# Whole-slot instructions, one root per store, pairwise adds and a 120-partition first piece in an fp32 pooling kernel

## Chip, cores, metric

One core of one Trainium2 chip. The metric is device time in microseconds (us), as the median of several executions. Ratios compare the mean time of one kernel's fast runs with that of the kernel before in the same rounds, so a ratio is not quite the ratio of the medians quoted next to it.

## The reference

For p = 2 and windows of 4 the reference is a root mean square over each window of the last axis:

```
x: float32 [32, 256, 4096]                   # 134.2 MB
window = np.abs(x[:, :, start:start + 4]) ** 2
result[:, :, i] = np.mean(window, axis=-1) ** (1 / 2)   # float32 [32, 256, 1024], 33.6 MB
```

## The kernel before

The input is seen as 128 partitions of 262144 columns. Three input slots of 13184 columns rotate. A slot is loaded by one transfer and worked in three chunks: ScalarE (ACT) squares a chunk in place, VectorE (DVE) sums each four neighbours, ACT takes the root of the chunk before. Two loads make one output group, which leaves by one store.

```python
    slots = [[(W, [4416, 4384, 4384])]] * 18
    ...
        for step in chunks:
            v = xs[i][:, c:c + step]
            nc.scalar.activation(out=v, in_=v, func=Act.Square)
            ...
            nc.vector.tensor_reduce(
                out=o, in_=v.rearrange("p (n j) -> p n j", j=k),
                axis=mybir.AxisListType.X, op=mybir.AluOpType.add,
            )
            if pending is not None:
                root(*pending)
```

Loads are issued by the sync queue (SP), stores of groups 0 to 6 by ACT's queue. The last four stores (g7 to g10) are held back to the end of SP's queue, so that they fill the DMA engines while the last loads are computed.

Of the kernel before, what the change touches and what calls it, by code (L numbers as in the profile page):

```python
# [1 line left out]

# [4 lines left out]


@with_exitstack
def kernel(  # L10
    ctx: ExitStack,
    tc: tile.TileContext,
    x: bass.AP,
    p: float,
    kernel_size: int,
    out: bass.AP,
):






    nc = tc.nc

    assert float(p) == 2.0, "kernel specialized for p == 2"
    k = int(kernel_size)
    assert k == 4, "kernel specialized for kernel_size == 4"

    P = nc.NUM_PARTITIONS  # L30
    fp32 = mybir.dt.float32
    Act = mybir.ActivationFunctionType
    xf = x.rearrange("b c l -> (b c l)")
    of = out.rearrange("b c l -> (b c l)")
    total = xf.shape[0] // P

    W, O_W = 13184, 6592
    X_SLOTS, O_SLOTS = 3, 2
    slots = [[(W, [4416, 4384, 4384])]] * 18
    slots += [[(6592, [3296, 3296])] * 2, [(6592, [3296, 3296]), (5056, [2528, 2528])]]  # L40
    groups = [2] * 9 + [3, 1]
    late = {7, 8, 9, 10}
    in_x = {9, 10}


    loads = [(s, sum(w for w, _ in slot[:j]), *slot[j]) for s, slot in enumerate(slots)
             for j in range(len(slot))]
    n = len(loads)
    assert sum(w for _, _, w, _ in loads) == total

    firsts = [sum(groups[:g]) for g in range(len(groups))]
    assert sum(groups) == n
    group_of = [g for g, count in enumerate(groups) for _ in range(count)]
    columns = [sum(w for _, _, w, _ in loads[firsts[g]:firsts[g] + groups[g]])
               for g in range(len(groups))]

    x_pool = ctx.enter_context(tc.tile_pool(name="x_pool", bufs=X_SLOTS))
    o_pool = ctx.enter_context(tc.tile_pool(name="o_pool", bufs=O_SLOTS))
    ctx.enter_context(tc.manual_schedule())

    def block(flat, g, div):
        at, width = sum(columns[:g]) * P // div, columns[g] * P // div
        return flat[at:at + width].rearrange("(p w) -> p w", p=P)

    slot_tiles = {}
    xs = {}

    def load(i):
        s, at, w, _ = loads[i]
        if at == 0:  # L70
            slot_tiles[s] = x_pool.tile([P, W], fp32, name="xt")
        v = slot_tiles[s][:, at:at + w]
        g = group_of[i]
        src = sum(loads[j][2] for j in range(firsts[g], i))
        nc.sync.dma_start(out=v, in_=block(xf, g, 1)[:, src:src + w])  # L75
        xs[i] = v

    ots = {}

    def store(g, queue):  # L80
        queue.dma_start(out=block(of, g, k), in_=ots[g])  # L81

    def root(g, o, ends):
        nc.scalar.activation(out=o, in_=o, func=Act.Sqrt, scale=1.0 / k)  # L84
        if ends and g not in late:
            store(g, nc.scalar)

    ahead = 0
    while ahead < n and loads[ahead][0] < X_SLOTS - 1:
        load(ahead)  # L90
        ahead += 1
    pending = None
    for i in range(n):
        s, _, w, chunks = loads[i]
        while ahead < n and loads[ahead][0] < s + X_SLOTS:
            load(ahead)
            ahead += 1
        g = group_of[i]
        if i == firsts[g]:
            pool, width = (o_pool, O_W) if g not in in_x else (x_pool, W)  # L100
            t = pool.tile([P, width], fp32, name="ot" if g not in in_x else "xt")
            ots[g] = t[:, 0:columns[g] // k]
        at = sum(loads[j][2] for j in range(firsts[g], i)) // k
        assert sum(chunks) == w
        c = 0
        for step in chunks:
            v = xs[i][:, c:c + step]
            nc.scalar.activation(out=v, in_=v, func=Act.Square)  # L108
            o = ots[g][:, at + c // k:at + (c + step) // k]
            nc.vector.tensor_reduce(  # L110
                out=o, in_=v.rearrange("p (n j) -> p n j", j=k),
                axis=mybir.AxisListType.X, op=mybir.AluOpType.add,
            )
            if pending is not None:
                root(*pending)
            c += step
            pending = (g, o, i == firsts[g] + groups[g] - 1 and c == w)
    root(*pending)
    for g in sorted(late):
        store(g, nc.sync)  # L120


# [1 line left out]
_INS = ['x', 'p', 'kernel_size']  # L124
_OUTS = [((32, 256, 1024), 'float32')]

_NUMBERS = {'p': 2.0, 'kernel_size': 4}


# [26 lines left out]
```

## Time and profile before

| | before |
|---|---|
| time | 394.69 us (394.66 to 394.81, 3 runs) |
| bytes moved | 167.8 MB in 390.0 us of transfers |
| plateau | 433 GB/s |
| DVE, ACT busy | 282.4 us, 292.4 us |

The page's row of DMA digits is the mean busy share of 16 DMA engines, so "9" in all inner slices means that there is little left to win. One thing the average hides is whether the 16 engines end together. The trace of the kernel before has 16 completions of each of its 33 transfers (528 four-byte packets); I read them as one for each of the 16 engines, but the trace does not say which engine a completion belongs to. For nearly every load of the steady stretch one engine completes about 0.5 us after the median engine, and at the last store 0.60 us after it (391.62 against 392.22 us). I call this distance the **lag**.

### The profile page before, as it was taken

How to read it: one execution, taken by the hardware profiler on the slowest of the kernel's cores; microseconds unless marked ns; L12 is line 12 of the kernel's file. 1: busy time of each engine (PE TensorE's matmuls, PEld its weight loads, DVE VectorE, ACT ScalarE, POOL GpSimd, SP SyncE). 2: the span in 40 equal slices, each digit the busy share in tenths (PEclk: the TensorE clock that was granted, in tenths of full speed). 3: DMA queues.
4: the chain of work that ended last, by engine and by line, in shares of the span. 5: the costliest groups of instructions: out<-in, count | busy, mean ns of one | idle time of the engine just before them, and what ended most of it. 6: DMA issues, size and time to landing. Idle time of an engine off the chain costs nothing.

```text
span 393.0 us, 316 instructions
## 1 busy us (share of the span) xinstructions
DVE 282.4 (72%) x62; ACT 292.4 (74%) x126; POOL 0.2 (0%) x4
## 2 busy tenths in 40 slices
DVE  0068989494959495949594959595859686899992
ACT  1099986777786768686958695959595949899991
POOL 0000000000000000000000000000000000000000
DMA  8999999999999999999999999999999999999997
GB/s 344 429 429 440 429 424 381 443 459 429 413 440 435 429 427 432 429 440 441 437 448 421 432 462 435 392 429 472 429 413 451 425 429 429 424 429 427 438 429 329
DMA packets 4754, 167.79 MB, mean 427 GB/s; under 512 B 528, under 2 KB 528, under 8 KB 656
## 3 DMA queue, kind: packets, MB, share of 16 engines
q1 hardware_dynamic: 3744, 144.15, 85.3%
q10 hardware_dynamic: 1008, 23.63, 14.0%
q14 instruction: 2, 0.02, 0.0%
HBM read 134.22 MB, written 33.55 MB: 427 GB/s over the span
## 4 chain that ended last, share of the span: by engine, by line
DMA 62%; ACT 19%; DVE 14%; issue 2%; ACTq 0%; SPq 0%
DMA xt<-in_x_dram 62%; ACT xt L108 15%; DVE ot L110 11%; DVE xt L110 3%; ACT ot L84 3%; ACT xt L84 1%; ACTq L81 0%; SPq L75 0%; ACTq L108 0%
## 5 line engine op out<-in xcount | busy, mean ns | idle before, releaser
L110 DVE TENSOR_REDUCE ot<-xt 128x1096 f32<-128x4384 f32 (+1 forms) x54 | 255.4, 4731 | 102.7 <-ACT xt L108 102.4
L108 ACT ACTIVATE xt<-xt 128x4384 f32<-128x4384 f32 (+3 forms) x62 | 230.3, 3716 | 89.2 <-DMA xt<-in_x_dram 86.3
L84 ACT ACTIVATE ot<-ot 128x1096 f32<-128x1096 f32 (+1 forms) x54 | 59.8, 1108 | 1.8 <-DVE ot L110 0.9
L110 DVE TENSOR_REDUCE xt<-xt 128x824 f32<-128x3296 f32 (+1 forms) x8 | 27.0, 3384 | 1.3 <-ACT xt L108 1.2
L84 ACT ACTIVATE xt<-xt 128x824 f32<-128x824 f32 (+1 forms) x8 | 6.7, 841 | 3.0 <-DVE xt L110 2.9
L108 ACT ACT_TABLE_LOAD x1 | 1.3, 1283 | 0.7 <-PEq L137 0.7
L84 ACT ACT_TABLE_LOAD x1 | 1.3, 1283 | 0.0
L137 POOL MEMSET const-bfloat16-1.0<- 128x1 bf16 x1 | 0.1, 101 | 0.0
L137 POOL MEMSET const-uint8-127<- 128x1 uint8 x1 | 0.1, 101 | 0.0
L137 POOL MEMSET const-float32-0.0<- 128x1 f32 x1 | 0.1, 98 | 0.2 <-issue 0.2
L137 POOL MEMSET const-float32-1.0<- 128x1 f32 x1 | 0.1, 98 | 0.0
## 6 DMA issues: line engine op xcount, KB each, us to landing
xt<-in_x_dram SPq DMA_DIRECT2D x18, 6592.0 KB, 39.7
out_dram<-ot ACTq DMA_DIRECT2D x7, 3296.0 KB, 26.4
xt<-in_x_dram SPq DMA_DIRECT2D x3, 3296.0 KB, 24.6
out_dram<-ot SPq DMA_DIRECT2D x2, 3296.0 KB, 29.6
xt<-in_x_dram SPq DMA_DIRECT2D x1, 2528.0 KB, 26.4
out_dram<-xt SPq DMA_DIRECT2D x1, 2472.0 KB, 9.3
out_dram<-xt SPq DMA_DIRECT2D x1, 632.0 KB, 5.0
```

Source lines behind the costliest of these rows:

```text
L84: nc.scalar.activation(out=o, in_=o, func=Act.Sqrt, scale=1.0 / k)
L108: nc.scalar.activation(out=v, in_=v, func=Act.Square)
L110: nc.vector.tensor_reduce(out=o, in_=v.rearrange("p (n j) -> p n j", j=k), axis=mybir.AxisListType.X, op=mybir.AluOpType.add,)
L137: nc = _bacc.Bacc("TRN2", target_bir_lowering=False, num_devices=1)
```

## The change

The intent is fewer, larger instructions and a short tail. Loads are squared and summed whole; one root is taken per store; from load 15 on, the sum is two pairwise adds, so that the coarse tail still ends in time; and 840 of the columns are laid on 120 partitions and loaded first, which spares one of the 16 DMA engines a little work. The core of the diff (cut; the rest gives tiles fixed addresses and moves offsets):

```diff
-    slots = [[(W, [4416, 4384, 4384])]] * 18
-    slots += [[(6592, [3296, 3296])] * 2, [(6592, [3296, 3296]), (5056, [2528, 2528])]]
+    slots = [[(W, [W])]] * 16 + [[(W, [6592, 6592])]] * 2
+    slots += [[(6592, [6592]), (6592, [6592])], [(6592, [6592]), (4216, [2112, 2104])]]
+    ODD = 840
...
+        if i < PAIRS:          # PAIRS = 15; the tensor_reduce of before
...
+        nc.vector.tensor_tensor(out=h, in0=q[:, :, 0:2], in1=q[:, :, 2:4], op=add)
+        nc.vector.tensor_tensor(out=o, in0=h[:, :, 0], in1=h[:, :, 1], op=add)
...
+    Q = 120
+    odd = ODD * P // Q
+    t = o_tiles[1][0:Q, 0:odd]
+    nc.sync.dma_start(out=t, in_=xf[(total - ODD) * P:total * P].rearrange("(p w) -> p w", p=Q))
...
+            if ends or i in FINE or (i in ENDS and c == w):
+                pending.append((done - 1, g, ots[g][:, rooted:summed], ends))
```

More of the change, by code (lines that the diff above doesn't have):

```diff
@@ L38 @@
     X_SLOTS, O_SLOTS = 3, 2
-    slots = [[(W, [4416, 4384, 4384])]] * 18
-    slots += [[(6592, [3296, 3296])] * 2, [(6592, [3296, 3296]), (5056, [2528, 2528])]]
+    slots = [[(W, [W])]] * 16 + [[(W, [6592, 6592])]] * 2
+    slots += [[(6592, [6592]), (6592, [6592])], [(6592, [6592]), (4216, [2112, 2104])]]
+    ODD = 840
     groups = [2] * 9 + [3, 1]
     late = {7, 8, 9, 10}
-    in_x = {9, 10}
+    in_x = {9: (2, 0), 10: (2, 4944)}
+    FINE, ENDS, LAG = {21}, {19, 20}, 1
+    PAIRS = 15
     loads = [(s, sum(w for w, _ in slot[:j]), *slot[j]) for s, slot in enumerate(slots)
@@ L48 @@
     n = len(loads)
-    assert sum(w for _, _, w, _ in loads) == total
+    assert sum(w for _, _, w, _ in loads) + ODD == total
     firsts = [sum(groups[:g]) for g in range(len(groups))]
@@ L55 @@
                for g in range(len(groups))]
-    x_pool = ctx.enter_context(tc.tile_pool(name="x_pool", bufs=X_SLOTS))
-    o_pool = ctx.enter_context(tc.tile_pool(name="o_pool", bufs=O_SLOTS))
+    x_pool = ctx.enter_context(tc.tile_pool(name="x_pool", bufs=1))
+    o_pool = ctx.enter_context(tc.tile_pool(name="o_pool", bufs=1))
+    x_tiles = [x_pool.tile([P, W], fp32, name=f"xt{j}") for j in range(X_SLOTS)]
+    o_tiles = [o_pool.tile([P, O_W], fp32, name=f"ot{j}") for j in range(O_SLOTS)]
     ctx.enter_context(tc.manual_schedule())
@@ L63, in block @@
         return flat[at:at + width].rearrange("(p w) -> p w", p=P)
-    slot_tiles = {}
     xs = {}
@@ L69, in load @@
         s, at, w, _ = loads[i]
-        if at == 0:
-            slot_tiles[s] = x_pool.tile([P, W], fp32, name="xt")
-        v = slot_tiles[s][:, at:at + w]
+        v = x_tiles[s % X_SLOTS][:, at:at + w]
         g = group_of[i]
@@ L86, in root, with total_sum @@
             store(g, nc.scalar)
+    def total_sum(o, v, i):
+        add = mybir.AluOpType.add
+        if i < PAIRS:
+            nc.vector.tensor_reduce(
+                out=o, in_=v.rearrange("p (n j) -> p n j", j=k),
+                axis=mybir.AxisListType.X, op=add,
+            )
+            return
+        q = v.rearrange("p (n j) -> p n j", j=k)
+        front = v[:, 0:v.shape[1] // 2]
+        h = front.rearrange("p (n j) -> p n j", j=2)
+        nc.vector.tensor_tensor(out=h, in0=q[:, :, 0:2], in1=q[:, :, 2:4], op=add)
[4 more added lines that the diff above has]
+    nc.sync.dma_start(out=t, in_=xf[(total - ODD) * P:total * P].rearrange("(p w) -> p w", p=Q))
     ahead = 0
-    while ahead < n and loads[ahead][0] < X_SLOTS - 1:
+    while ahead < n and loads[ahead][0] < X_SLOTS:
         load(ahead)
         ahead += 1
-    pending = None
+    nc.vector.tensor_tensor(out=t, in0=t, in1=t, op=mybir.AluOpType.mult)
+    o = o_tiles[1][0:Q, odd:odd + odd // k]
+    nc.vector.tensor_reduce(
+        out=o, in_=t.rearrange("p (n j) -> p n j", j=k),
+        axis=mybir.AxisListType.X, op=mybir.AluOpType.add,
+    )
+    nc.scalar.activation(out=o, in_=o, func=Act.Sqrt, scale=1.0 / k)
+    nc.scalar.dma_start(
+        out=of[(total - ODD) * P // k:total * P // k].rearrange("(p w) -> p w", p=Q), in_=o,
+    )
+    pending = []
+    done = 0
     for i in range(n):
@@ L99 @@
         if i == firsts[g]:
-            pool, width = (o_pool, O_W) if g not in in_x else (x_pool, W)
-            t = pool.tile([P, width], fp32, name="ot" if g not in in_x else "xt")
-            ots[g] = t[:, 0:columns[g] // k]
-        at = sum(loads[j][2] for j in range(firsts[g], i)) // k
+            t, first = (o_tiles[g % O_SLOTS], 0) if g not in in_x else (x_tiles[in_x[g][0]], in_x[g][1])
+            ots[g] = t[:, first:first + columns[g] // k]
+            summed = rooted = 0
         assert sum(chunks) == w
@@ L108 @@
             nc.scalar.activation(out=v, in_=v, func=Act.Square)
-            o = ots[g][:, at + c // k:at + (c + step) // k]
-            nc.vector.tensor_reduce(
-                out=o, in_=v.rearrange("p (n j) -> p n j", j=k),
-                axis=mybir.AxisListType.X, op=mybir.AluOpType.add,
-            )
-            if pending is not None:
-                root(*pending)
-            c += step
-            pending = (g, o, i == firsts[g] + groups[g] - 1 and c == w)
-    root(*pending)
+            total_sum(ots[g][:, summed:summed + step // k], v, i)
+            while pending and pending[0][0] <= done - LAG:
+                root(*pending.pop(0)[1:])
+            done += 1
+            c += step
+            summed += step // k
+            ends = summed == columns[g] // k
+            if ends or i in FINE or (i in ENDS and c == w):
+                pending.append((done - 1, g, ots[g][:, rooted:summed], ends))
+                rooted = summed
+    for job in pending:
+        root(*job[1:])
     for g in sorted(late):
```

## The prediction

The 27 GB/s of one engine are 52736 bytes in 1947 ns, the median packet of the kernel before.

For squares and reduces, a straight line through two shapes of the kernel before is an estimate: squares of 3296 and 4384 took 2933 and 3843 ns, so 13184 takes 11.20 us, 6592 5.69 and 2112 1.94; reduces of the same two sizes took 3586 and 4719 ns, so 13184 takes 13.88 us. Roots are put on the line of the squares (6592: 5.69 us, 3296: 2.93, 1648: 1.56). How long an add takes was the author's estimate, since the kernel before has none; the two adds of 13184 inputs then took 7.03 + 3.59 = 10.62 us.

> **What bounds the kernel now.** I read the page first, then the DMA row in windows, then the groups by form, then the waits of the queue that issues loads, then the timeline of the tail.
>
> The page:
>
> ```profile
> span 393.0 us, 316 instructions
> DVE 282.4 (72%) x62; ACT 292.4 (74%) x126; POOL 0.2 (0%) x4
> DMA  8999999999999999999999999999999999999997
> HBM read 134.22 MB, written 33.55 MB: 427 GB/s over the span
> ```
>
> Neither compute engine is above 74%, while the DMA row is full in every slice but the first and last. The page's chain of waits gives DMA only 62% and puts ACT and DVE at 33% together. That must not be read as "a third of the time is compute": the chain follows one buffer through square, reduce, next load, while the other buffers keep the DMA engines busy. The stage table tells it better (from:to in us, then length, busy time of DVE, ACT, POOL, clock, DMA share, GB/s):
>
> ```profile
> 20.00:56.00 36.00, 29.68 (x7) 33.72 (x14) 0.00 (x0) 1.00 1.01 435
> 56.00:64.00 8.00, 7.44 (x2) 7.96 (x3) 0.00 (x0) 1.00 0.95 356
> 64.00:340.00 276.00, 201.63 (x44) 205.83 (x87) 0.00 (x0) 1.00 1.00 433
> 340.00:380.00 40.00, 37.69 (x10) 38.73 (x19) 0.00 (x0) 1.00 1.01 433
> 380.00:393.00 13.00, 5.92 (x3) 4.44 (x4) 0.00 (x0) 1.00 0.81 348
> ```
>
> The plateau is 433 GB/s with share 1.00. Three places fall below it: the start, 56 to 64 us (the first store begins at 55.6), and the last microseconds. I now count what can be won at all. 167.77 MB at 433 GB/s take 387.5 us. The packet records start at 1.7 us and end at 391.7 us, so transfers are under way for 390.0 us, and 2.5 us of that is loss. The first store's dent is some 1.0 to 1.4 of it (8 us x (1 - 356/433) = 1.4; packets are booked where they start, so a window's edge is worth some tenths). The rest is the slow first packets and engines that don't end together. The 1.7 us ahead, the 1.3 us after the last packet, and the 1.7 us between span (393.0) and measured time (394.69) belong to launch and completion; the change doesn't touch them. So **perfect transfers would give 394.7 - 2.5 = 392.2 us, a gain of 0.6%.**
>
> Of the compute rows I need the durations by shape, and the queue's waits:
>
> ```profile
> L110 DVE TENSOR_REDUCE ot<-xt 128x1096 f32<-128x4384 f32 x36 | 169.9, 4719 | 6.7 <-ACT xt L108 6.4
> L108 ACT ACTIVATE xt<-xt 128x4384 f32<-128x4384 f32 x36 | 138.3, 3843 | 2.9 <-ACT ot L84 2.9
> L84 ACT ACTIVATE ot<-ot 128x1096 f32<-128x1096 f32 x36 | 39.7, 1103 | 1.1 <-DVE ot L110 0.9
> ...
> SPq L75 <- DVE ot L110: 307.7, 17, 18.7
> ```
>
> The load queue waits 17 times for a reduce to free a slot. This is harmless as long as the other two slots are still filling when the next load is issued.
>
> The tail in the timeline:
>
> ```profile
> 381.39 6.11 SPq L81 DMA_DIRECT2D out_dram<-xt  x2
> 386.42 0.73 ACT L84 ACTIVATE xt<-xt 128x632 f32<-128x632 f32 x1 [2.23 <-DVE xt L110]
> ```
>
> The last two stores are issued at 381.4 and, after the last root, at 387.2 us. Both are queued while earlier stores still drain, so the DMA does not run dry.
>
> [...]
>
> **The change part by part.**
>
> *Whole-slot instructions.* [...]Fewer fixed costs: ACT's squares and roots go from 124 to 39, [...]all on an engine that is not the bound. The cost is grain. A slot comes free 11.2 + 13.9 = **25.1 us** after landing, against 3.9 + 3 x 4.75 = 18 us and some before. With three slots the next load must be queued before the two loads behind it end, the earliest 2 x 6.75 MB / 433 = 31.2 us after landing. Issue to first packet is about 1.0 us (0.73 to 1.74 at the start). Margin: 31.2 - 25.1 - 1.0 = **5 us**, more while a store shares the engines. So no gap.
>
> *One root per store.* Root g is behind the square of the next group's first load, and starts 11.2 us after that landing. The store goes out about 17 us after it, 12 later than before. With 26.4 us to landing (page's issue row) the output tile is free at 43; it is wanted again two groups on, at 39.3 (two loads and a store) + 11.2 = 50.5 us. Margin 7 us. ACT per pair of loads: 2 x 11.2 + 5.7 = 28 of 39.3 us.
>
> *Pairwise adds from load 15.* [...]This only speeds up the tail, whose grain is now coarse. ACT sets the tail: load 16 should land near 323 us (324.1 was its first square before). From there ACT has four squares of 6592, a root of g7 and of g8 and three more squares of 6592: 9 x 5.68; then a root of 3296 (2.9) and a square of 2112 (1.95): 56.0 us, to 379. The add of load 20 ends then too, its root takes 1.6: store 9 at **381**, as before. The fine last pieces end near 385.5, against 387.2. Needed: behind store 8 remain 5998 columns x 512 B = 3.07 MB = 7.1 us, so it must be issued by 391.3 - 7.1 - 1.0 = 383. Margin 2 us.
>
> *The odd piece.* 840 columns are 430 KB in and 107 KB out. Spread over 15 engines, the sixteenth carries 33.6 KB less, which at 27 GB/s is 1.25 us; each other one 2.2 KB more, 0.08 us. The trace has a reason for it: by 3.1 us only 15 packets have started, the sixteenth starts at 3.2, a microsecond after the others, and completions of the first load spread over 1.3 us. That engine is probably the one spared. It then starts with the second issue, some 0.4 us later: relief 1.25 - 0.4 - 0.08 = 0.8 us against a lag of 0.6 to 0.9. Per-packet cost is 2 x 978 - 1947 = 9 ns from the packet records; 16 more packets are 0.14 us. Its small square, reduce and root (some 2.7 us) fall into compute's idle first 19 us. Its early store may also take over part of the first-store dent at 56 us, whose cause I can't see.
>
> **Sum.** Engines ending together: -0.4 (completions of the last store spread over 1 us, the mean 0.6 before the last, not all of it curable). Dent: -0.4, a guess between 0 and -1. More packets: +0.14. Compute: 0. So 394.7 - 0.7 = **394.0 us**.
>
> **The rivals.** *Slots come back late.* Whole-slot grain leaves the load queue dry. For it: 307.7 us of waits on a reduce, and a slot return 7 us later. Against: 5 us of margin. If I were wrong by 1 us beyond it per load, it would show some 19 times: about 413 us, slower. *Pairwise adds slow or ACT late in the tail.* If strided two-input adds ran at half rate, load 20's add would end 5 us later and store 9 miss its mark by 3: 397 us. Against: [...]DVE is behind ACT anyway. *The whole loss goes:* balanced ends and no dent, 392.2 to 393. *The dent is paid twice* or the small first piece hinders the start: 395.
>
> **Range and chances.** The floor, 392.2, is the hard side; the tail's 2 us margin is the soft one. 8 in 10: 393.1 to 395.0. Faster by 2% means below 386.8, under the floor: 0.005. Slower by 2% needs repeated gaps, above 402.6: 0.015. Within 2%: 0.98.
>
> **What would show it.** Right: plateau still 433 GB/s from 64 to 380 us, DVE near 263 us, ACT near 281, adds of 6592 outputs at 7.0 us, one table load fewer, the last load landing near 369, store 9 issued near 381. Completions of the last store closer together shows the balance. Wrong: zeros in the DMA row, load waits that end after the slot before has landed, or output tiles awaited by the reduce.

## The result

| | before | after |
|---|---|---|
| median of 6 runs | 394.87 us (394.66 to 394.98) | 394.73 us (394.23 to 395.50) |
| ratio | | 1.0000 (95%: 0.9987 to 1.0012) |
| span of the profiled run | 393.0 us | 392.8 us |
| DVE, ACT busy | 282.4, 292.4 us | 263.2, 279.8 us |

The change is worth nothing that can be measured. The page of the changed kernel:

```profile
span 392.8 us, 203 instructions
DVE 263.2 (67%) x37; ACT 279.8 (71%) x40; POOL 0.2 (0%) x4
DMA  9999999899999999999899999999999999999997
HBM read 134.22 MB, written 33.55 MB: 427 GB/s over the span
```

DVE lost 19 us of work and ACT 13, and the span lost 0.2: the DMA row is as full as it was, with the same 427 GB/s. The table of stages has the same columns as the one in the prediction:

```profile
20.00:56.00 36.00, 22.62 (x2) 26.76 (x3) 0.00 (x0) 1.00 0.98 423
56.00:64.00 8.00, 6.30 (x2) 8.00 (x2) 0.00 (x0) 1.00 0.98 422
64.00:340.00 276.00, 195.49 (x18) 200.25 (x23) 0.00 (x0) 1.00 1.00 432
340.00:380.00 40.00, 32.96 (x13) 38.70 (x9) 0.00 (x0) 1.00 1.01 432
380.00:392.80 12.80, 3.63 (x4) 4.42 (x4) 0.00 (x0) 1.00 0.82 351
```

The plateau did not move. The dent (the fall below the plateau at the first store) seems gone from 56 to 64 us, but it only moved with the first large store, which now starts at 68.4 us. I summed by how much each 52736-byte packet exceeds the undisturbed 1947 ns. Per engine that is 0.98 us between 56 and 64 us before, and 0.67 us between 68 and 76 plus 0.23 near 148 after. The groups by form:

```profile
L96 DVE TENSOR_REDUCE ot<-xt 128x3296 f32<-128x13184 f32 x15 | 208.3, 13885 | 95.0 <-ACT xt L143 95.0
L143 ACT ACTIVATE xt<-xt 128x13184 f32<-128x13184 f32 x16 | 179.0, 11190 | 88.0 <-DMA xt<-in_x_dram 86.3 <-ACT ot L89 1.7
L105 DVE TENSOR_TENSOR xt<-xt 128x6592 f32<-128x6592 f32 x1 | 7.0, 7025 | 3.3 <-ACT xt L143 3.3
```

and the load queue's waits (total, times, longest):

```profile
SPq L80 <- DVE ot L96: 302.1, 15, 43.0
```

Every duration is within 0.03 us of the prediction (13.9, 11.2, 7.0). The load queue waits for reduces as long as it did (302 against 308 us), and still as harmlessly as far as the DMA row shows. In the tail's timeline, the last two stores start at 381.4 (predicted 381), and the last root ends at 385.95 (predicted near 385.5):

```profile
381.43 4.88 SPq L86 DMA_DIRECT2D out_dram<-xt  x2
...
385.31 0.64 ACT L89 ACTIVATE xt<-xt 128x526 f32<-128x526 f32 x1 [1.53 <-DVE xt L106]
```

**Where the small expected gain went.** This is the ledger of the two profiled runs (394.78 and 394.83 us), from the completions in the two traces:

| | before | after | difference |
|---|---|---|---|
| median engine completes the last store | 391.62 | 391.52 | -0.10 |
| lag of the last engine | 0.60 | 0.33 | -0.27 |
| last completion | 392.22 | 391.85 | -0.37 |
| from there to the end of the span | 0.79 | 0.92 | +0.13 |
| from the span to the measured time | 1.77 | 2.06 | +0.29 |

The last completion did come earlier, by 0.37 us, and then the way from it to the end of the measured time became 0.42 us longer. The median engine gained only 0.10 because the busy time of the DMA engines did not fall (390.14 and 390.22 us per engine). Slow large packets cost 0.63 us less than before. But the odd piece (the 840 columns on 120 partitions) takes 1.66 us per engine to load and 0.31 to store, while the shorter last load and last store give back only 0.98 and 0.23.

The last two rows are no chance of one profile. From the completion to the end of the span it is 0.79 us in all five profiles without an odd piece and 0.92 in e2_before_odd, which only adds one. From the span to the measured time it is 1.90 to 2.13 us in the six executions of the changed kernel, and 1.73 to 1.83 in the 27 of the kernel before that ran beside the experiments.

### The profile page after: what moved, and what is told of

The parts are those of the page before. It is cut to its first block, busy times and chain, and to the rows that moved or that the text cites. A ratio compares the mean times of both kernels' runs of the same rounds, so it can differ in the third digit from the quotient of the medians.

```text
span 392.8 us, 203 instructions
## 1 busy us (share of the span) xinstructions
DVE 263.2 (67%) x37; ACT 279.8 (71%) x40; POOL 0.2 (0%) x4
## 4 chain that ended last, share of the span: by engine, by line
DMA 47%; ACT 27%; DVE 16%; issue 7%; SPq 0%; ACTq 0%
DMA xt<-in_x_dram 47%; ACT xt L143 21%; DVE ot L96 14%; ACT ot L89 6%; DVE xt L105 1%; DVE xt L106 1%; ACT xt L89 1%; ACTq L86 0%; SPq L80 0%; SPq L112 0%; ACTq L89 0%
## 5 line engine op out<-in xcount | busy, mean ns | idle before, releaser
L143 ACT ACTIVATE xt<-xt 128x13184 f32<-128x13184 f32 (+3 forms) x25 | 222.4, 8909 | 98.2 <-DMA xt<-in_x_dram 96.5
L96 DVE TENSOR_REDUCE ot<-xt 128x3296 f32<-128x13184 f32 x15 | 208.3, 13885 | 95.0 <-ACT xt L143 95.0
L89 ACT ACTIVATE ot<-ot 128x6592 f32<-128x6592 f32 x9 | 51.1, 5681 | 0.0
L105 DVE TENSOR_TENSOR xt<-xt 128x3296 f32<-128x3296 f32 (+3 forms) x10 | 34.7, 3468 | 22.0 <-ACT xt L143 21.7
L106 DVE TENSOR_TENSOR ot<-xt 128x1648 f32<-128x1648 f32 (+1 forms) x5 | 11.1, 2218 | 0.2
L89 ACT ACTIVATE xt<-xt 128x3296 f32<-128x3296 f32 (+3 forms) x4 | 5.8, 1449 | 2.3 <-DVE xt L106 2.3
L106 DVE TENSOR_TENSOR xt<-xt 128x1648 f32<-128x1648 f32 (+2 forms) x5 | 7.0, 1408 | 0.2
L117 DVE TENSOR_TENSOR ot<-ot 120x896 f32<-120x896 f32 x1 | 1.1, 1092 | 4.7 <-DMA ot<-in_x_dram 4.7
L119 DVE TENSOR_REDUCE ot<-ot 120x224 f32<-120x896 f32 x1 | 1.1, 1085 | 0.0
```

The costliest lines, as they stand in the source:

```text
L89: nc.scalar.activation(out=o, in_=o, func=Act.Sqrt, scale=1.0 / k)
L96: nc.vector.tensor_reduce(out=o, in_=v.rearrange("p (n j) -> p n j", j=k), axis=mybir.AxisListType.X, op=add,)
L105: nc.vector.tensor_tensor(out=h, in0=q[:, :, 0:2], in1=q[:, :, 2:4], op=add)
L106: nc.vector.tensor_tensor(out=o, in0=h[:, :, 0], in1=h[:, :, 1], op=add)
L117: nc.vector.tensor_tensor(out=t, in0=t, in1=t, op=mybir.AluOpType.mult)
L119: nc.vector.tensor_reduce(out=o, in_=t.rearrange("p (n j) -> p n j", j=k), axis=mybir.AxisListType.X, op=mybir.AluOpType.add,)
```

## The experiments

All runs gave the right result. "Lag" is at the last store of the profiled run. Runs of one block shared a chip and the runs of the kernel before (medians 394.83, 394.90 and 394.86 us).

| run | median, us | ratio to before (95%) | lag, us |
|---|---|---|---|
| before | 394.83 to 394.90 | 1 | 0.60 |
| after | 394.73 | 1.0000 (0.9987 to 1.0012) | 0.33 |
| e1_no_odd | 395.68 | 1.0018 (1.0006 to 1.0031) | 2.16 |
| e2_before_odd | 394.66 | 0.9992 (0.9980 to 1.0005) | 0.56 |
| e3_odd_128 | 395.63 | 1.0022 (1.0008 to 1.0036) | 0.73 |
| e4_odd_second | 397.61 | 1.0067 (1.0055 to 1.0080) | 1.29 |
| e5_idle_piece | 395.26 | 1.0009 (0.9997 to 1.0022) | 0.55 |
| e6_odd_double | 395.87 | 1.0022 (1.0009 to 1.0034) | 0.38 |
| e7_no_pairs | 399.97 | 1.0125 (1.0111 to 1.0139) | 0.21 |
| e8_more_dve | 398.75 | 1.0100 (1.0084 to 1.0115) | 1.25 |
| e9_no_odd_again | 396.01 | 1.0028 (1.0014 to 1.0042) | 2.37 |
| e10_late_store | 395.74 | 1.0027 (1.0014 to 1.0039) | 0.08 |
| e11_fine_one_root | 394.81 | 0.9999 (0.9987 to 1.0012) | 1.07 |
| e12_odd_half | 395.76 | 1.0027 (1.0013 to 1.0041) | 1.18 |

After the result my theory was: the change's compute parts cost nothing, the odd piece levels the engines' ends, and its own packets eat that gain. The rival: the coarse parts (whole-slot instructions, late stores, pairwise adds) cost some tenths, and the odd piece wins them back. By "grain" I mean how much of a slot one instruction works.

### e1_no_odd, and e9_no_odd_again (the same kernel, a second time)

```diff
-    slots += [..., [(6592, [6592]), (4216, [2112, 2104])]]
-    ODD = 840            # and the first piece's load, work and store
+    slots += [..., [(6592, [6592]), (5056, [2528, 2528])]]
```

> The changed kernel without the odd piece; its 840 columns go back into the last load (5056 columns, 128 partitions). Theory (the odd piece halves the spread of completions, worth 0.4 us at the end, and costs about as much at the start through its small packets): completions of the last store spread over 0.9 us again, first load's packets pay the start once, time 394.5 to 394.9, the same as both kernels within 0.3. Rival (coarse grain, late stores or pairwise adds cost some tenths that the odd piece wins back): time over 395.2.

> The same kernel as e1_no_odd, again, for a second profile. If the late engine is a property of this kernel: last engine of the last store some 2 us behind the median again, time 395.4 to 396.0. If it was chance in one profile: 0.6 us behind, and the time is owed to something else.

The two gave 395.68 and 396.01 us. My theory missed and the rival held: without the odd piece the coarse kernel is 0.2 to 0.3% slower than the kernel before. Both profiles show the same picture in the last microseconds. These are the DMA rows of a window from 391.5 to 394 us (40 slices of 0.06 us; one engine of 16 shows as 0 or 1), first before, then e1_no_odd:

```profile
DMA  2000000000000000000000000000000000000000
GB/s 81 0 0 0 0 0 0 0 0 0 0 0 0 0 0 0 0 0 0 0 0 0 0 0 0 0 0 0 0 0 0 0 0 0 0 0 0 0 0 0
DMA packets 3, 0.01 MB, mean 2 GB/s; under 512 B 2, under 2 KB 2, under 8 KB 3
```

```profile
DMA  1001001001001001001000000000000000000000
GB/s 81 0 0 81 0 0 81 0 0 81 0 0 81 0 0 81 0 0 81 0 0 0 0 0 0 0 0 0 0 0 0 0 0 0 0 0 0 0 0 0
DMA packets 8, 0.04 MB, mean 14 GB/s; under 512 B 1, under 2 KB 1, under 8 KB 8
```

In e1_no_odd one single engine is still writing its rows of the last store, one packet every 0.19 us, while the 15 others have ended. The median engine is even 0.4 us earlier than in the kernel before (391.23 against 391.62). The lag is 0.68 us until the first large store, 1.26 at 86 us, and 2.33 at 165 us. In the repeat it is 0.98, 1.59 and 2.45 at the same places, so it belongs to this kernel and is no chance of one profile.

### e2_before_odd

```diff
-    slots += [..., [(6592, [3296, 3296]), (5056, [2528, 2528])]]
+    slots += [..., [(6592, [3296, 3296]), (4216, [2112, 2104])]]
+    ODD = 840            # first piece on 120 partitions, as in the changed kernel
```

> The kernel before with the odd piece alone added, 840 columns on 120 partitions as first transfer, last load 4216. Theory: spread at the end falls from 0.96 to about 0.5 us, packets of the odd piece take some 0.6 us per engine more than their bytes are worth, time 394.5 to 394.9. Rival (the odd piece is a pure gain, something else in the change spends it): 394.2 to 394.4.

394.66 us, as the theory had it, but the expected narrowing at the end did not come: the lag is 0.56 us in place of 0.60. The ratio's interval includes 1, so in the fine-grained kernel the odd piece is worth nothing that can be told from noise.

### e3_odd_128

```diff
-    Q = 120
+    Q = 128
```

> The changed kernel with the odd piece laid on 128 partitions of 840 columns, so on 16 engines. Theory (the spared engine is what evens the ends): spread of completions 0.9 us as before, and the cost of small first packets stays, so 0.3 to 0.5 us slower than the changed kernel: 395.0 to 395.2. Rival (any small piece ahead of the loads evens the ends): spread 0.5, time unchanged at 394.7.

395.63 us: some 0.9 slower than with 120 partitions (other rounds, the same kernel before), and level with e1_no_odd in the same block (395.68). By the time, then, the piece that leaves an engine out (15 completion packets, against 16 for this one) is the one that pays. The profile is less clear: the lag is 0.73 us, far below the 2.16 of e1_no_odd, so this piece evens the engines too, and 0.37 us of it is lost again after the last completion (2.98 against 2.61 us). This profile is of the run's fastest execution (395.23), that of e1_no_odd of its slowest (396.00), so how much of it is real is not known.

The packets also tell the price of the 120 partitions. On 128 partitions the piece's 3360-byte packets have a median of 132 ns and a mean of 174, slow ones mostly at the start. On 120 partitions the 3584-byte packets have a median of 170 and a mean of 221 in the changed kernel (medians of 142 to 170 over the five profiles that begin with them): nearly half take 140 ns, but those started after 3.1 us have a median of 200.

### e4_odd_second

```diff
-    nc.sync.dma_start(out=t, in_=xf[...])     # odd piece
-    ahead = 0
+    ahead = 1
+    load(0)
+    nc.sync.dma_start(out=t, in_=xf[...])     # odd piece
```

> The changed kernel with the odd piece issued behind the first big load in place of ahead of it. Theory (its packets were slow because they were the first): odd packets near their undisturbed 138 ns, spread still 0.5 us, first big packets pay the start once, 0.3 us faster than the changed kernel: about 394.4. Rival (the odd piece costs the same wherever it is): unchanged at 394.7.

397.61 us: wrong, for both. The cause was mine. The odd piece's root stands first in ACT's program, so the first square now waits for the odd piece (timeline of e4_odd_second):

```profile
24.07 0.39 ACT L124 ACTIVATE ot<-ot 120x224 f32<-120x224 f32 x1 [22.07 <-DVE ot L120]
...
25.18 11.19 ACT L144 ACTIVATE xt<-xt 128x13184 f32<-128x13184 f32 x1 [0.72 <-ACT ot L124]
```

In the changed kernel that square started at 20.41. The first slot comes back as much later, load 3 is issued at 50.3 us in place of 45.5, and 19 large packets from 48 to 56 us run slow, 0.55 us per engine. Fourteen more run slow from 16 to 20 us, beside the odd piece, another 0.54. The late engine makes up most of the rest (lag 1.29). The theory's premise failed too: behind a large load the odd packets took 195 ns on average, not 138, so being first is only a part of what makes them slow. Most of the first 52 took 140 ns, the later ones about 235.

### e5_idle_piece

```diff
     # e1_no_odd, and:
+    t = o_tiles[1][0:120, 0:896]
+    nc.sync.dma_start(out=t, in_=xf[total * P - 120 * 896:total * P].rearrange("(p w) -> p w", p=120))
```

> The run without the odd piece (e1_no_odd, 395.68 us), with a first load of 430 KB on 120 partitions added whose data nobody uses: 0.26% more bytes, all of them on 15 engines. Theory (one late engine sets the end of that run, 1.6 us behind the next, and 15 others have slack): the extra megabytes are free or nearly so, 395.6 to 396.1, and the completions of the last store lie closer together than the 2.4 us of e1_no_odd. Rival (all engines end together in effect and every byte counts): 430 KB at 433 GB/s more, 396.7.

395.26 us, below even the theory's range, and the rival's 396.7 is refuted: the kernel moves 0.43 MB more than e1_no_odd and is 0.4 us faster, though of two different blocks (ratios 1.0009 against 1.0018 and 1.0028). The lag fell from over 2 us to 0.55. So what the piece does, it does by its transfer; its data does not matter. How it evens the engines is seen at the start. Before, 15 engines start their first large packet from 1.74 to 2.28 us and one at 3.19; in the changed kernel all 16 start theirs from 3.32 to 3.93. So the piece delays the 15 rather than starting one early. That the engine left out is the late one is likely, but not shown, since the trace does not name engines.

### e6_odd_double and e12_odd_half

```diff
-    ODD = 840
+    ODD = 1680      # e6_odd_double, last load 3376
+    ODD = 420       # e12_odd_half, last load 4636
```

> The changed kernel with an odd piece of twice the size (1680 columns; the last load is 3376). The spared engine then has 67 KB less, 2.5 us. Theory (the relief of 840 columns already brings the late engine level): the others carry 0.08 us more each, 394.7 to 394.9. Rival (more relief still pays): 394.0 to 394.4.

> The changed kernel with half the odd piece, 420 columns. The relief falls to 17 KB, 0.6 us, and the cost of its packets, which take up to twice as long as on 128 partitions, to half. Theory (relief of a late engine against doubled packets, with no odd piece at 395.68, 840 columns at 394.73, 1680 at 395.87): between, 394.8 to 395.3, last engine 0.4 to 0.9 us behind the median. Rival (840 is too much already): 394.3 to 394.6.

395.87 and 395.76 us: both slower than with 840, and outside what I had expected of them. With twice the size the lag is good (0.38), but the median engine completes at 392.30, 0.8 us later. The packet records say why: its 7168-byte packets take 484 ns on average, where 7168 bytes at the pace of the large packets would take 265. They slow down under way: those started from 2.5 to 3.0 us have a median of 272 ns, those after 5 us of 546. The piece costs 3.63 us per engine. With half the size the packets have a median of 74 ns, which is their pace, so the doubled packets of my theory did not come (the doubling shows with 840 columns: the last twelve packets on 120 partitions took 140 to 274 ns in the changed kernel, the last 38 on 128 in e3_odd_128 at most 132); the median engine is early (391.21), but now two engines trail by 1.2 us. So 840 is the best of the three sizes tried, and I can't compute it from the relief in bytes alone.

### e7_no_pairs

```diff
-    PAIRS = 15
+    PAIRS = 22
```

> The changed kernel with the one-instruction reduce to the end, no pairwise adds. Worked from the measured durations: a reduce of 6592 takes 7.02 us in place of 5.47, the root of g8 then waits for the add of load 17 until 361, the last squares move by 4 us, store 9 is issued at 388.0 in place of 381.4, and the transfers must have it by about 383. Theory: DMA gap near 384 to 389, time up by 4.8 us, 399.5. Rival (the tail's slack hides it): 394.7.

399.97 us, so 5.1 over before in the same rounds, where 4.8 was worked out. Of the parts of the change, this is the one whose removal moves the time most. Timeline of the tail, and the DMA row from 380 to 396 us (slices of 0.4 us), without the pairwise adds:

```profile
388.48 5.23 SPq L86 DMA_DIRECT2D out_dram<-xt  x2
```

```profile
DMA  3949939403000000000000090909899290909099
```

The same row of the changed kernel:

```profile
DMA  9493979919698999999696957994000000000000
```

Store 9 is issued at 388.5 in place of 381.4 us, and no packet starts from 384.0 to 389.2 us (thirteen zeros). The pairwise adds do not make the kernel faster than before; they repair what the coarse grain would break in the tail.

### e8_more_dve

```diff
         if i < PAIRS:
             nc.vector.tensor_reduce(out=o, in_=..., axis=..., op=add)
+            quarter = v.shape[1] // 4
+            nc.vector.tensor_reduce(out=o[:, 0:quarter // k], in_=v[:, 0:quarter]..., op=add)
             return
```

> The changed kernel with a quarter of each of the first 15 reduces done twice: 15 x 3.6 us more work on DVE, results unchanged. Theory (compute is off the path while slots come back within 31.2 - 1.0 us of landing): a slot comes back after 28.7 us, DVE busy near 316 us, time unchanged at 394.7. Rival (slots already come back too late, the load queue runs dry): some 3.6 us per load, up to 448.

398.75 us, 4.0 more than the changed kernel, with DVE busy for 316.5 us as expected. My theory that the slots had room was wrong by its size: the rival's mechanism is there, though not at each load. The stretch from 48 to 85 us, around the first large store, shows it; first the changed kernel, then e8_more_dve:

```profile
DMA packets 368, 15.66 MB, mean 423 GB/s; under 512 B 32, under 2 KB 32, under 8 KB 32
```

```profile
DMA packets 326, 14.45 MB, mean 391 GB/s; under 512 B 32, under 2 KB 32, under 8 KB 32
```

Load 3 is issued at 49.3 us in place of 45.5, some 2 us before the load ahead of it completes, and load 4 at 66.7. In this stretch the DMA engines idle 0.8 us on average; over the whole run they are 1.8 us longer busy, in slow large packets; and the lag grows by 0.9. That is 3.5 of the 4.0 us.

### e10_late_store

```diff
-            if pending is not None:
-                root(*pending)
+            while len(pending) > (3 if i < 16 else 0):
+                root(*pending.pop(0))
```

> The kernel before with each root, and so each store, held back by two more chunks until load 16: stores start some 15 us after a load lands, as in the changed kernel, while slots come back as early as before. If the time of the stores makes the kernel without the odd piece slower: 395.3 to 395.8 and a last engine 1.5 to 2 us late. If not: 394.6 to 395.0 and 0.6 us late.

395.74 us, in the range of "stores matter", but the profile says that this is not why. The lag stays at 0.5 to 0.6 us to the end of the loads. The time was lost in the tail: the held-back roots delay ACT, store 9 goes out at 384.88, and in the DMA row from 380 to 396 us no packet starts from 383.2 to 385.6:

```profile
384.88 6.11 SPq L81 DMA_DIRECT2D out_dram<-xt  x2
```

```profile
DMA  9997799300000090919899290909099990000000
```

So the run is flawed as a test of the time, and it did not hold the slots' return fixed either: its reduces waited six times, 69.0 us in all, for output tiles whose store had not landed. It does show that late stores do not by themselves make one engine late: its first one went out at 71.05 us, against 55.6 in the kernel before and 68.67 in e1_no_odd.

### e11_fine_one_root

```diff
     # e1_no_odd, with
-    slots = [[(W, [W])]] * 16 + ...
+    slots = [[(W, [4416, 4384, 4384])]] * 16 + ...
```

> The kernel without the odd piece (e1_no_odd), with squares and adds of the first 16 loads cut in three again and one root per store kept: slots come back early as in the kernel before, stores start some 10 us after a load lands. If late slots make e1_no_odd slower: back to 394.6 to 395.0. If one late root per store does: 395.4 to 396.0.

394.81 us. Squares and adds in three chunks, with one root per store, no odd piece, and pairwise adds kept, is level with the kernel before. It is 0.9 to 1.2 us faster than e1_no_odd and e9_no_odd_again, which differ from it in the chunks of the first 16 loads alone; e9_no_odd_again shared its block. So the whole-slot grain is what costs, and one root per store costs nothing that can be measured. The row from 391.5 to 394 us has no trail of packets (compare e1_no_odd above):

```profile
DMA  1000000000000000000000000000000000000000
DMA packets 2, 0.01 MB, mean 2 GB/s; under 512 B 1, under 2 KB 1, under 8 KB 2
```

Its last engine completes at 392.24 us, as in the kernel before (392.22). The lag (1.07) is larger only because the median engine is earlier (391.18).

## Why the prediction was right or wrong

- **What bounds the kernel: right.** 32 us less compute left the 433 GB/s plateau and the time where they were. No kernel of the study came out measurably faster than the kernel before.
- **Durations, slot return, tail: right.** The first slot came back 25.2 us after its load (20.38 to 45.54), predicted 25.1. Store 9 was within 0.5 us, and e7_no_pairs confirmed the tail's working to 0.3 us. The last load landed at 369.06 us (predicted near 369), and one table load went, as predicted (two of 1.28 us before, one after).
- **"Margin: 5 us ... So no gap": right for the changed kernel, too generous as a rule.** I counted a load in time if it was issued 1.0 us before the one ahead of it completes. e8_more_dve and e4_odd_second issue load 3 only about 2 us before that, and the engines already run slow (large packets by 0.55 us per engine in e4_odd_second). In the changed kernel it was 5.9 us.
- **"Compute: 0": wrong by about 1 us, and hidden.** The term was mis-sized, and another one covered it. Whole-slot grain costs 0.9 to 1.2 us (e11_fine_one_root against e1_no_odd and e9_no_odd_again), not by a gap but, in both profiles, by one late engine.
- **Engines ending together, -0.4: right in direction.** The lag fell by 0.27 us. (The last completion, which holds all terms together, came 0.37 earlier where 0.7 was predicted.) But the term's value depends on the kernel. In the coarse kernel the odd piece wins 0.9 to 1.3 us (394.73 against 395.68 and 396.01, across blocks); in the fine one nothing that can be measured. The cost of the grain and the gain of the odd piece cancel.
- **"It then starts with the second issue, some 0.4 us later: relief ... 0.8 us": wrong.** No engine starts a large packet before 3.32 us in the changed kernel, 2.1 us after that issue began. Its ground was weak as well: of the six profiles that open with a large load, the latest first packet starts at anything from 2.39 to 3.19 us, and in e1_no_odd two engines are late together. One engine a microsecond behind was the picture of one profile.
- **Its packets, +0.14: mis-sized.** I counted only 9 ns per packet. The small pieces cost a net 0.76 us per engine (1.66 + 0.31 - 0.98 - 0.23). The per-packet cost was as worked out (undisturbed, these packets take 140 ns, 8 more than their bytes at the pace of the large ones); the other 0.6 is packets that run slower than that. On 128 partitions (e3_odd_128) that excess is 0.33 us, so the 120 partitions explain only a part of it. Slow large packets gave 0.63 back.
- **Dent, -0.4: wrong in these two profiles.** It was called a guess: 0.98 us became 0.90. Whether a small early store can take it over is not shown. In the 10 us after the first large store is issued, slow large packets cost 0.00 to 1.25 us per engine in the eight profiles with such an early store, and 0.34 to 0.99 in the six without.
- **"The change doesn't touch" launch and completion: wrong.** There are 0.42 us more between the last completion and the end of the measured time, 0.13 of it with the odd piece; the cause of the rest stays open.

Below, the range held because the floor of 392.2 us left no room. Above, it held by luck: the grain alone would have brought 395.7 to 396.0 us, outside the range, and an odd piece worth more than twice its predicted term made up for it. The centre, 0.7 us too low, came from a sum whose terms were each a few tenths, and most of them were off.

**What stays open.** Why whole-slot grain makes one engine late. It falls behind at the first large store and again near 150 to 165 us, in both profiles of that kernel, and late stores by themselves don't do it (e10_late_store). e8_more_dve, where the slots come back later still and the lag is 1.25 in place of 0.33 us, points to the late slots; no run parts them from the size of the instructions. Also open is why half an odd piece leaves two engines behind.

## What to carry to other kernels

When the DMA row is full, work out the floor from bytes and plateau first: here it capped the gain at 0.6% before any part of the change was looked at. Then look at the 16 completions one by one, since the mean hides the last: in e1_no_odd it came 2.16 us after the median. Coarser instructions on an engine that was "not the bound" still delayed the return of buffers here, from 18.6 to 25.2 us for the first slot. So measure how early the next transfer is queued: with load 3 issued about 2 us ahead (e4_odd_second) the large packets already ran slow, by 0.55 us per engine, and with 5.9 us (the changed kernel) by 0.01.

## What else the traces show

- The load on 120 partitions has 15 four-byte completion packets, the one on 128 (e3_odd_128) 16. Packets on 120 partitions slowed down in the course of a transfer: of 7168 bytes (e6_odd_double), a median of 272 ns for those started from 2.5 to 3.0 us and 546 after 5 us; the last 38 of the 3360-byte packets on 128 partitions all took at most 132. No run here separates the cause.
- With load 3 issued 5.9 us ahead of the end of the transfer before it, the large packets from 48 to 56 us took their normal time (0.01 us per engine too long); with about 2 us (e4_odd_second) they did not (0.55).
- In the kernel before, the first packet started 0.63 us after the issuing instruction ended (1.11 to 1.74), the sixteenth at 3.19 us (2.39 to 3.16 in five other profiles), and the first sixteen 52736-byte packets took 2220 to 3039 ns instead of 1947.
- The time after the last completion differs between two kernels of the same work: 2.56 us before and 2.98 after. Over the 14 profiles, span to measured time was 1.77 to 1.78 us where no program text was fetched after the span, and 1.78 to 2.06 where some was. That is a correlation, not a test.
